# Retention's gate projected by tokens, and group norm's gains applied before the turn

## The chip, the cores and the metric

The kernel runs on one core of a Trainium2 chip. The metric is the device time of one execution in microseconds (us). Engines are named as in the profile: PE is TensorE's matmuls, PEld its weight loads, DVE VectorE, ACT ScalarE, POOL GpSimd, SP SyncE, whose queue issues nearly all transfers.

## The reference

Two layers over 256 tokens of width 1024 in float32. Each layer runs three token mixers side by side on a normalised input (MLA, MoBA and retention), merges them through sigmoid gates, multiplies by an output matrix and adds the result to the input; then comes a squared-ReLU MLP. Retention, which the change touches, is cut to this:

```python
p = h @ w_in                       # rq, rk, rv, rg are columns of p
...
o = (inner + cross).reshape(B, H, S, Dv)          # H = 4 heads, Dv = 128
mu = jnp.mean(o, axis=-1, keepdims=True)
var = jnp.mean(jnp.square(o - mu), axis=-1, keepdims=True)
o = (o - mu) * lax.rsqrt(var + GN_EPS)
o = o.transpose(0, 2, 1, 3).reshape(B, S, RET_V_W) * gn_w + gn_b
return jax.nn.silu(g) * o                         # g is rg, 512 columns
...
sigmoid(g_ret) * (o_ret @ w_branch_ret)
```

## The kernel before

**Data.** The 256 tokens are two tiles of 128 (t = 0, 1). The normalised input xn lies with the 1024 features along partitions, in 8 pieces k of 128. Every float32 product of weights is made of three fp32r products (`three`, L215): both operands are split into a high and a low part, and high x high, high x low and low x high are added in PSUM. Weights come from memory in blocks of 512 KB (`raw`, 4 buffers, issued on SP's queue at L180); ACT copies the high part (`whi`, L195), DVE subtracts for the low part (`wlo`, L197), 6 buffers each. `weight_plan` fixes the order of the blocks.

**Two ways to project.** `project` holds a 128 x 128 piece of xn still and moves 512 columns of weights: the result has tokens along partitions, one PSUM bank (`acc`, 4 of them) for each token tile. `project_t` holds a piece of weights still and moves the 256 tokens: the result has features along partitions. Retention's gate (`rg_unit`) uses `project_t`, in four blocks of 128 columns, two to a PSUM bank.

**Retention, in the order of the program.** The projections rqk and rv; the turns and scores of the heads (`ret_turn`, `ret_scores`); the gate rg, between whose four units the scores and values (`ret_values`, into the PSUM tiles `por`) are set; then the MoBA branch (bmoba0, bmoba1), with `group_norm` behind its second unit; then the gates gret0 and gret1, with `oret_turn` behind their first two units; then the retention branch bret0, bret1. `group_norm` normalises by tokens into `oret` (L826). `oret_turn` transposes it on PE (L840), so that features lie along partitions, applies the group norm's weight and offset there, a scalar for each partition (L844), multiplies by the gate (L845), and splits the result into high and low (L235, L236) for bret. The gate itself is scaled by the tokens' inverse norm laid along the free axis (`xn.row`, L861), passed through tanh (L862) and completed to silu (L863; the factor 0.5 is in L845).

**Order.** The program is a list of units (`prog`) with steps hung behind them (`at`, `slot`). A scheduler with a timeline of its own then orders the instructions of each engine, except where the code holds an engine to the program's order (`manual_schedule`, `keep_in_program_order`). Each engine executes its list in order. The SBUF buffer `KK` holds the MLA keys, and in the last layer also the final norm's gains `gf`.

Of the kernel before, what the change touches and what calls it, by code (L numbers as in the profile page):

```python
# [7 lines left out]
F32 = mybir.dt.float32  # L8
F32R = mybir.dt.float32r
AF = mybir.ActivationFunctionType  # L10
ALU = mybir.AluOpType
AX = mybir.AxisListType

P = 128
D = 1024
S = 256
NT = S // P
L = 2
KD = D // P
# [10 lines left out]
RT_H, RT_K, RT_V = 4, 64, 128  # L30
# [4 lines left out]
C_RQK, C_RV, C_RG = range(1952, 2464), range(2464, 2976), 2976  # L35
# [10 lines left out]
def weight_plan():  # L46

    plan = []

    def block(key, name, kt, cols, per):  # L50
        for j in range(0, kt, per):
            plan.append(((*key, j // per), name, (j, per), cols))

    def span(c, n):
        return range(c, c + n)

    for l in range(L):
        if l == 0:

            plan.append(((l, "b0", 0), "w_in", (0, 1), C_MLA))  # L60
            plan.append(((l, "mq", 0), "w_in", (0, 1), C_MQ))
            for k in range(1, KD):
                plan.append(((l, "b0mq", k), "w_in", (k, 1), range(0, 928)))
        else:
            block((l, "b0"), "w_in", KD, C_MLA, 2)
            block((l, "mq"), "w_in", KD, C_MQ, 2)
        block((l, "mk"), "w_in", KD, C_MK, 2)
        block((l, "mv"), "w_in", KD, C_MV, 2)
        mv, plan = plan[-4:], plan[:-4]
        for i, (key, name, kt, cols) in enumerate(  # L70
            (("qrope", "mla_w_q_up", 2, C_QROPE), ("qnope", "mla_w_q_up", 2, C_QNOPE), ("kvup", "mla_w_kv_up", 1, C_KV))
        ):
            block((l, key), name, kt, cols, kt)
            plan.append(mv[i])
        plan.append(mv[3])
        for i in range(2):
            block((l, "gmla%d" % i), "w_in", KD, span(C_GMLA + 512 * i, 512), 2)
        for i in range(2):
            block((l, "gmoba%d" % i), "w_in", KD, span(C_GMOBA + 512 * i, 512), 2)
        for i in range(2):  # L80
            block((l, "bmla%d" % i), "w_branch_mla", 4, span(512 * i, 512), 2)
        block((l, "rqk"), "w_in", KD, C_RQK, 2)
        block((l, "rv"), "w_in", KD, C_RV, 2)
        for n in range(4):
            block((l, "rg", n), "w_in", KD, span(C_RG + P * n, P), KD)
        for i in range(2):
            block((l, "bmoba%d" % i), "w_branch_moba", 4, span(512 * i, 512), 2)
        for i in range(2):
            block((l, "gret%d" % i), "w_in", KD, span(C_GRET + 512 * i, 512), 2)
        for i in range(2):  # L90
            block((l, "bret%d" % i), "w_branch_ret", 4, span(512 * i, 512), 2)
        for n in range(KD):
            block((l, "wout", n), "w_out", KD, span(P * n, P), KD)
        for f in range(0, NF + 2, 2):
            for i in (f, f + 1) if f < NF else ():
                block((l, "up", i), "w_mlp_up", KD, span(P * i, P), KD)
            for i in (f - 2, f - 1) if 2 <= f <= NF - ENDS else ():
                plan.append(((l, "down", i, 0), "w_mlp_down", (i, 1), range(D)))
        for i in range(NF - ENDS, NF):
            plan.append(((l, "down", i, 0), "w_mlp_down", (i, 1), range(D)))  # L100
    at, offset = {}, 0
    for key, name, (j, n), cols in plan:
        at[key] = (offset, n, len(cols))
        offset += P * n * len(cols)
    return plan, at, offset
# [14 lines left out]

G_ATT, G_MLP = 0, L * KD
G_CQ = 2 * L * KD
G_GN = G_CQ + L * 3
G_END = G_GN + L * 2 * RT_H


@with_exitstack
def trunk(ctx: ExitStack, tc: tile.TileContext, gx, wts, consts, gfin, xtok, out):


    nc = tc.nc
# [4 lines left out]
    sb = ctx.enter_context(tc.tile_pool(name="sb", bufs=1))  # L136
# [66 lines left out]
    def acc_tile(name="acc"):  # L203
        return ps.tile([P, 512], F32, name=name, tag="acc", bufs=4)
# [4 lines left out]
    def w2k(name):  # L209
        return sb.tile([P, 512], F32, name=name, tag="w2k", bufs=W2K)  # L210
# [9 lines left out]
    def gain(c):  # L220
        return G[:, c : c + 1]

    def halves(tile_):
        return tile_.rearrange("p (two s) -> p two s", two=2)
# [9 lines left out]
    def split_plain(src, hi, lo):  # L234
        nc.scalar.activation(hi, src, AF.Copy)  # L235
        nc.vector.tensor_sub(lo, src, hi.bitcast(F32))  # L236
# [119 lines left out]
    def project_t(l, key, n, xn, o):  # L356

        wh, wl = load_w(l, key, n, 0)
        for k in range(KD):
            xh, xl = xn.k(k)  # L360
            three(o, wh[:, k, :], wl[:, k, :], xh, xl, k == 0, k == KD - 1)
# [166 lines left out]
    xn = Normed(G_ATT)  # L528
# [21 lines left out]
    prog, steps = [], {}  # L550

    def at(slot, step):
        steps.setdefault(slot, []).append(step)

    def slot(key, j):
        return [k for k, _ in prog].index((key, j))
# [9 lines left out]
    def layer(l, xn, before):  # L566

        c0 = []
        c, mla, mqkv, rqkv = {}, {}, {}, {}
# [161 lines left out]
        omlaT, omobaT, oretT = [], [], []  # L731
# [50 lines left out]

            return done

        rT, or_ps, aT, rg, oret = [], [], {}, [], []

        def ret_turn(i):
            pt = misc_tile("prt")
# [23 lines left out]
        def group_norm():  # L812
            for t in range(NT):
                o = w2k("oret")
                oret.append(o)
                st = sb.tile([P, RT_H, 6], F32, name="gst", bufs=2)
                mv = sb.tile([P, RT_H, 2], F32, name="gmv", bufs=2)
                ve = small("gve")
                for h in range(RT_H):
                    nc.vector.bn_stats(st[:, h, :], or_ps[t][:, RT_V * h : RT_V * h + RT_V])  # L820
                    nc.vector.bn_aggr(mv[:, h, :], st[:, h, :])
                nc.vector.tensor_scalar(ve[:, 0:RT_H], mv[:, :, 1], GN_EPS, None, op0=ALU.add)
                nc.gpsimd.tensor_tensor(ve[:, RT_H : 2 * RT_H], ve[:, 0:RT_H], neghalf[:, 0:RT_H], op=ALU.pow)
                for h in range(RT_H):
                    cs = slice(RT_V * h, RT_V * h + RT_V)
                    nc.vector.tensor_scalar(  # L826
                        o[:, cs], or_ps[t][:, cs], mv[:, h, 0:1], ve[:, RT_H + h : RT_H + h + 1],
                        op0=ALU.subtract, op1=ALU.mult,
                    )

        def oret_turn(i):
            if i == 0:
                oretT.extend((t4("oreth"), t4("oretl")))
            pt = misc_tile("pot")
            y = w2k("oy")
            for kk in range(2):
                k = 2 * i + kk
                cs = slice(S * kk, S * kk + S)
                for t in range(NT):
                    nc.tensor.transpose(  # L840
                        pt[:, (2 * kk + t) * P : (2 * kk + t + 1) * P], oret[t][:, P * k : P * k + P], ident
                    )
                g = G_GN + 2 * RT_H * l + k
                nc.vector.tensor_scalar(y[:, cs], pt[:, cs], gain(g), gain(g + RT_H), op0=ALU.mult, op1=ALU.add)  # L844
            nc.vector.scalar_tensor_tensor(y, y, 0.5, rg[i], op0=ALU.mult, op1=ALU.mult)  # L845
            split_plain(y, *(o[:, 2 * i : 2 * i + 2, :].rearrange("p k s -> p (k s)") for o in oretT))

        project(l, "rqk", xn, 512, ret_done("rqk"))
        project(l, "rv", xn, 512, ret_done("rv"))


        rg_acc = []

        def rg_unit(n):
            if n % 2 == 0:
                rg_acc.append(acc_tile())
            acc = rg_acc[-1]
            project_t(l, "rg", n, xn, acc[:, S * (n % 2) : S * (n % 2) + S])
            if n % 2:
                z, th = w2k("rg"), w2k("tg")  # L860
                nc.vector.tensor_mul(halves(z), halves(acc), xn.row[:, None, :].to_broadcast([P, 2, S]))  # L861
                nc.scalar.activation(th, z, AF.Tanh, scale=0.5)  # L862
                nc.vector.scalar_tensor_tensor(z, th, 1.0, z, op0=ALU.add, op1=ALU.mult)  # L863
                rg.append(z)

        for n in range(RT_H):
            prog.append((("rg", n), lambda n=n: rg_unit(n)))
        branch(l, "bmoba", omobaT, th_moba, merged)
        th_ret = gates(l, "gret", xn)
        order_out = ExitStack()  # L870
# [67 lines left out]
        accs = [acc_tile() for _ in range(4)]  # L938
# [56 lines left out]
        for f in range(0, NF, 2):  # L995
# [5 lines left out]
            for g in (f - 2, f - 1) if 2 <= f <= NF - ENDS else ():  # L1001
                w = load_w(l, "down", g, 0)
# [16 lines left out]
        if not last:  # L1019
            xn = Normed(G_ATT + KD * (l + 1))  # L1020
# [41 lines left out]
        for t in range(NT):  # L1062
            y = sb.tile([P, D], F32, name="y", tag="t4", bufs=T4)
# [11 lines left out]
            else:  # L1075

                sl, more = slice(P, 2 * P), misc_tile("plast")
                for half, o in enumerate((accs[3], more)):
                    cs = slice(512 + 256 * half, 768 + 256 * half)
# [18 lines left out]
                op0=ALU.add, op1=ALU.add,  # L1098
# [5 lines left out]
            if t:  # L1104
                nc.vector.scalar_tensor_tensor(y[:, cs], xr[:, t, cs], r, gf[:, 0, cs], op0=ALU.mult, op1=ALU.mult)
                cs = slice(512, 768)
            else:
                cs = right
# [105 lines left out]
```

## Time and profile before

| | |
|---|---|
| time, median of 3 runs | 844.61 us (844.55 to 844.74) |
| the profiled execution: its own time, its span | 844.61 us, 842.8 us |
| granted TensorE clock, mean | 0.999 |
| PE, DVE, ACT busy | 99%, 72%, 59% of the span |
| matmuls, DVE instructions, ACT instructions | 4555, 1187, 867 |
| moved by DMA | 150.08 MB |

Busy time of PE includes the drain of each matmul, so matmuls in a row overlap in the records; the distance between two starts is what one costs. The waits of an engine list what it waited for, in total, how often and at longest. The chain of waits is the work that ended last, followed back from the end. The busy time by stretch gives, for a window of the span, the busy time and count of each engine, the granted clock, the share of the DMA engines and the GB/s they moved.

### The profile page before, as it was taken

The page shows a single profiled execution, that of the slowest core. Times are in us where ns is not written, and L with a number is a line of the kernel's source. Part 1 is how long each engine was busy: PE and PEld are TensorE (multiplying, and loading weights), DVE is VectorE, ACT ScalarE, POOL GpSimd, SP SyncE. Part 2 cuts the span into 40 slices and gives each one's busy share as a digit, 9 for nine tenths or more (in the row PEclk, how much of TensorE's full clock was granted, in tenths as well). Part 3 has the DMA queues.
Part 4 walks back from the last instruction along what each step waited for, and adds up shares of the span by engine and source line. Part 5 has one row for each costly group of instructions (what it writes and reads, how often), then busy time and mean ns, then how long its engine had stood idle before and what let it go on. Part 6 is the DMA issues. An engine that isn't in the chain of part 4 may idle for free.

```text
span 842.8 us, 12495 instructions
## 1 busy us (share of the span) xinstructions
PE 834.7 (99%) x4555; PEld 717.5 (85%) x4555; DVE 606.1 (72%) x1187; ACT 498.7 (59%) x867; POOL 14.4 (2%) x23
## 2 busy tenths in 40 slices
PE   9999999999999999999999999999999999999996
PEld 7888888988998888888888888879889988888886
DVE  7887787787777666666588868867878766556664
ACT  7757766535556555555677667654456555555552
POOL 0000000010000000000000000000100000000000
PEclk9999999999999999999999999999999999999999
DMA  9765444545456656665366545455565565666641
GB/s 355 255 208 183 129 144 153 171 151 183 146 175 222 200 193 185 197 191 182 118 207 220 174 139 164 138 163 155 171 186 161 181 204 184 184 199 184 191 126 51
DMA packets 42397, 150.08 MB, mean 178 GB/s; under 512 B 4704, under 2 KB 5088, under 8 KB 42336
## 3 DMA queue, kind: packets, MB, share of 16 engines
q1 hardware_dynamic: 41760, 148.42, 56.0%
q8 instruction: 36, 0.59, 0.3%
q10 hardware_dynamic: 576, 0.87, 0.3%
q14 instruction: 25, 0.20, 0.1%
HBM read 148.22 MB, written 1.05 MB: 177 GB/s over the span
## 4 chain that ended last, share of the span: by engine, by line
PE 98%; issue 1%; DMA 0%; DVE 0%; ACT 0%; POOLq 0%; POOL 0%; DVEq 0%
PE acc L216 20%; PE acc L217 20%; PE acc L218 20%; PE pup L955 13%; PE pup L957 7%; PE acc L906 5%; PE ps_pt L433 1%; PE ps_s L739 1%; PE po L460 1%; PE ps_s L400 1%; PE acc L632 0%; PE acc L635 0%; PE acc L633 0%; PE po L462 0%; PE pmt L878 0%
## 5 line engine op out<-in xcount | busy, mean ns | idle before, releaser
L197 DVE TENSOR_TENSOR wlo<-raw,whi 128x1024 fp32r<-128x1024 f32 (+3 forms) x286 | 336.9, 1184 | 164.2 <-ACT whi L195 100.7
L195 ACT ACTIVATE whi<-raw 128x1024 fp32r<-128x1024 f32 (+3 forms) x286 | 292.4, 1026 | 197.4 <-PE acc L218 92.5
L216 PE MATMUL acc<-whi,xs 128*128 128x512 f32 (+1 forms) x352 | 139.5, 398 | 0.0
L217 PE MATMUL acc<-wlo,xs 128*128 128x512 f32 (+1 forms) x352 | 138.5, 393 | 0.0
L218 PE MATMUL acc<-whi,xs 128*128 128x512 f32 (+1 forms) x352 | 138.3, 394 | 0.0
L955 PE MATMUL pup<-xs,whi 128*128 128x512 f32 x496 | 121.5, 391 | 0.0
L955 PEld LDWEIGHTS pup<-xs,whi 128*128 128x128 f32 x496 | 92.2, 188 | 18.6
L216 PE MATMUL acc<-whi,sq 128*128 128x512 f32 (+1 forms) x256 | 99.8, 390 | 0.0
L217 PE MATMUL acc<-wlo,sq 128*128 128x512 f32 (+1 forms) x256 | 99.6, 389 | 0.0
L218 PE MATMUL acc<-whi,sq 128*128 128x512 f32 (+1 forms) x256 | 98.4, 388 | 0.0
L218 PEld LDWEIGHTS acc<-whi,xs 128*128 128x128 f32 x352 | 66.2, 188 | 12.9 <-issue 0.2
L216 PEld LDWEIGHTS acc<-whi,xs 128*128 128x128 f32 x352 | 66.1, 188 | 12.7 <-issue 0.2
L217 PEld LDWEIGHTS acc<-wlo,xs 128*128 128x128 f32 x352 | 66.3, 188 | 12.0 <-issue 0.2
L957 PE MATMUL pup<-xs,wlo 128*128 128x256 f32 x496 | 68.5, 283 | 0.0
L957 PEld LDWEIGHTS pup<-xs,wlo 128*128 128x128 f32 x496 | 65.8, 191 | 2.9
L966 ACT ACTIVATE relu<-relu 128x256 f32<-128x256 f32 x64 | 25.8, 409 | 55.1 <-DVE relu L965 55.1
L218 PEld LDWEIGHTS acc<-whi,sq 128*128 128x128 f32 x256 | 48.0, 188 | 9.9
L216 PEld LDWEIGHTS acc<-whi,sq 128*128 128x128 f32 x256 | 48.2, 188 | 9.1
L217 PEld LDWEIGHTS acc<-wlo,sq 128*128 128x128 f32 x256 | 48.2, 188 | 8.8
L422 ACT ACTIVATE prob<-prob,smx 128x128 f32<-128x128 f32 x64 | 28.4, 445 | 11.5 <-DVE smx L419 11.1
L906 PE MATMUL acc<-mTh,whi 128*128 128x256 f32 x128 | 32.0, 286 | 0.0
L906 PE MATMUL acc<-mTh,wlo 128*128 128x256 f32 x128 | 31.7, 283 | 0.0
(276 smaller groups left out, 1192.8 us busy)
## 6 DMA issues: line engine op xcount, KB each, us to landing
raw<-wts SPq DMA_DIRECT2D x264, 512.0 KB, 3.9
raw<-wts SPq DMA_DIRECT2D x7, 464.0 KB, 7.2
raw<-wts SPq DMA_DIRECT2D x4, 416.0 KB, 3.3
xrow<-xtok SPq DMA_DIRECT2D x4, 256.0 KB, 8.3
raw<-wts SPq DMA_DIRECT2D x3, 256.0 KB, 4.0
DEC<-consts SPq DMA_DIRECT2D x1, 768.0 KB, 7.1
x<-gx SPq DMA_DIRECT2D x1, 512.0 KB, 6.4
gf<-gfin SPq DMA_DIRECT2D x1, 512.0 KB, 4.4
```

The source lines that it names most:

```text
L195: nc.scalar.activation(hi[:, cs], raw[:, cs], AF.Copy)
L197: nc.vector.tensor_sub(lo[:, cs], raw[:, cs], hi[:, cs].bitcast(F32))
L216: nc.tensor.matmul(o, ah, bh, start=start, stop=False)
L217: nc.tensor.matmul(o, ah, bl, start=False, stop=False)
L218: nc.tensor.matmul(o, al, bh, start=False, stop=stop)
L400: nc.tensor.matmul(o, b if swap else a, a if swap else b, start=i == 0, stop=i == 1)
L422: nc.scalar.activation(p[:, a:b], p[:, a:b], AF.Exp, bias=m[:, 2 + i : 3 + i], scale=scale, accum_out=m[:, 4 + i : 5 + i])
L433: nc.tensor.transpose(pt[:, P * i : P * i + P], got["p"][:, src : src + P], ident)
L906: nc.tensor.matmul(acc[:, :S], a, b, start=i == 0 and ks[0] == 0, stop=i == len(jobs) - 1 and ks[-1] == KD - 1)
L955: nc.tensor.matmul(u, w, xm.both(k), start=k == 0, stop=False)
L957: nc.tensor.matmul(u[:, 0:S], w, xm.k(k)[0], start=False, stop=k == KD - 1)
L966: nc.scalar.activation(s, s, AF.Square)
```

## The change

The gate rg is projected by `project`: xn's pieces are held still and its 512 columns of weights move, so that the gate has tokens along partitions. Its weights come in the same four blocks of 512 KB, cut along k in place of columns. tanh reads the accumulator itself, with the token's inverse norm as a scalar for each partition. The group norm's weights and offsets come as a row of 1024 values repeated on all partitions, one transfer of 512 KB a layer into the buffer `KK`, issued behind the first unit of rqk. `group_norm` multiplies by the weights, adds the offsets and applies the gate (the factor 0.5 is in `xn.halfcol`), all by tokens. `oret_turn` only transposes and splits.

```diff
-        for n in range(4):
-            block((l, "rg", n), "w_in", KD, span(C_RG + P * n, P), KD)
+        block((l, "rg"), "w_in", KD, span(C_RG, 512), 2)
...
-G_GN = G_CQ + L * 3
-G_END = G_GN + L * 2 * RT_H
+G_END = G_CQ + L * 3
...
         def group_norm():
...
+                w, b = rg["gn"][:, 0:512], rg["gn"][:, 512:1024]
+                nc.vector.tensor_mul(o, o, w)
+                nc.vector.tensor_add(o, o, b)
+                nc.vector.scalar_tensor_tensor(o, o, xn.halfcol[t], rg[t], op0=ALU.mult, op1=ALU.mult)
 
         def oret_turn(i):
...
-            y = w2k("oy")
...
-                g = G_GN + 2 * RT_H * l + k
-                nc.vector.tensor_scalar(y[:, cs], pt[:, cs], gain(g), gain(g + RT_H), op0=ALU.mult, op1=ALU.add)
-            nc.vector.scalar_tensor_tensor(y, y, 0.5, rg[i], op0=ALU.mult, op1=ALU.mult)
-            split_plain(y, *(o[:, 2 * i : 2 * i + 2, :].rearrange("p k s -> p (k s)") for o in oretT))
+            split_plain(pt, *(o[:, 2 * i : 2 * i + 2, :].rearrange("p k s -> p (k s)") for o in oretT))
...
-        rg_acc = []
-
-        def rg_unit(n):
-            if n % 2 == 0:
-                rg_acc.append(acc_tile())
-            acc = rg_acc[-1]
-            project_t(l, "rg", n, xn, acc[:, S * (n % 2) : S * (n % 2) + S])
-            if n % 2:
-                z, th = w2k("rg"), w2k("tg")
-                nc.vector.tensor_mul(halves(z), halves(acc), xn.row[:, None, :].to_broadcast([P, 2, S]))
-                nc.scalar.activation(th, z, AF.Tanh, scale=0.5)
-                nc.vector.scalar_tensor_tensor(z, th, 1.0, z, op0=ALU.add, op1=ALU.mult)
-                rg.append(z)
-
-        for n in range(RT_H):
-            prog.append((("rg", n), lambda n=n: rg_unit(n)))
+        def rg_done(accs):
+            for t in range(NT):
+                z = rg[t] = w2k("rg")
+                nc.scalar.activation(z, accs[t], AF.Tanh, scale=xn.halfcol[t])
+                nc.vector.scalar_tensor_tensor(z, z, 1.0, accs[t], op0=ALU.add, op1=ALU.mult)
+
+        def load_gn():
+
+            rg["gn"] = sb.tile([P, 2 * RT_H * RT_V], F32, name="gn", tag="KK", bufs=1)
+            src = bass.AP(tensor=gn.tensor, offset=gn.offset + 1024 * l, ap=[[0, P], [1, 1024]])
+            tc.keep_in_program_order(nc.sync.dma_start(rg["gn"], src))
+
+        project(l, "rg", xn, 512, rg_done)
+        at(slot("rqk", 0), load_gn)
```

More of the change, by code (lines that the diff above doesn't have):

```diff
@@ L122, with trunk @@
 G_CQ = 2 * L * KD
-G_GN = G_CQ + L * 3
-G_END = G_GN + L * 2 * RT_H
+G_END = G_CQ + L * 3
 @with_exitstack
-def trunk(ctx: ExitStack, tc: tile.TileContext, gx, wts, consts, gfin, xtok, out):
+def trunk(ctx: ExitStack, tc: tile.TileContext, gx, wts, consts, gfin, gn, xtok, out):
     nc = tc.nc
@@ L783, in ret_done @@
             return done
-        rT, or_ps, aT, rg, oret = [], [], {}, [], []
+        rT, or_ps, aT, rg, oret = [], [], {}, {}, []
         def ret_turn(i):
@@ L834, in oret_turn @@
             pt = misc_tile("pot")
-            y = w2k("oy")
             for kk in range(2):
                 k = 2 * i + kk
-                cs = slice(S * kk, S * kk + S)
                 for t in range(NT):
@@ L1195 @@
         gains[:, G_CQ + 3 * l + 2] = a["mla_kv_norm"][l]
-        for i, name in enumerate(("ret_gn_w", "ret_gn_b")):
-            c = G_GN + (2 * l + i) * RT_H
-            gains[:, c : c + RT_H] = a[name][l].reshape(RT_H, P).T
     arrays = {
@@ L1204 @@
         "gfin": np.ascontiguousarray(a["final_norm"]),
+        "gn": np.stack([a["ret_gn_w"], a["ret_gn_b"]], axis=1),
         "xtok": np.ascontiguousarray(a["x"].reshape(NT, P, D).transpose(1, 0, 2)),
```

## The prediction

> **What bounds the kernel now.** I read the page first, then the waits of PE, then the chain of waits, then the busy time by stretch.
>
> ```profile
> span 842.8 us, 12495 instructions
> PE 834.7 (99%) x4555; PEld 717.5 (85%) x4555; DVE 606.1 (72%) x1187; ACT 498.7 (59%) x867; POOL 14.4 (2%) x23
> PE 98%; issue 1%; DMA 0%; DVE 0%; ACT 0%; POOLq 0%; POOL 0%; DVEq 0%
> PE warm L548 <- DVE zero L155: 1.4, 1, 1.4
> 156.00:171.40 15.40, 15.40 (x132) 15.36 (x131) 11.66 (x20) 8.37 (x11) 0.00 (x0) 1.00 0.50 168
> 182.00:206.00 24.00, 24.00 (x111) 19.67 (x110) 20.05 (x38) 11.67 (x13) 2.32 (x2) 1.00 0.60 197
> ```
>
> The first three lines say that the chain is TensorE almost alone. The fourth is the only line that the waits of PE contain: after the first 1.4 us PE never waits. The last two are stretches of layer 0 (length, then busy PE, PEld, DVE, ACT, POOL, granted clock, DMA share, GB/s): the gate's projection, and the group norm's stage. PE is busy through them at full clock, DVE 20 of 24 us. So the time is the sum of PE's issue intervals, and what the change does on DVE, ACT and the DMA queue counts only if it makes PE wait.
>
> A matmul's recorded duration includes its drain, so I price one by the distance between starts. In order of time:
>
> ```profile
> 156.15 0.28 PE L216 MATMUL acc<-xs,whi 128*128 128x256 f32 x1
> 158.90 0.28 PE L218 MATMUL acc<-xs,wlo 128*128 128x256 f32 x1
> 159.60 0.28 PE L217 MATMUL acc<-xs,whi 128*128 128x256 f32 x1
> L218 PE MATMUL acc<-xs,wlo 128*128 128x256 f32 x32 | 9.2, 286 | 0.0
> 183.06 0.39 PE L216 MATMUL acc<-whi,xs 128*128 128x512 f32 x1
> 188.50 0.39 PE L216 MATMUL acc<-whi,xs 128*128 128x512 f32 x1
> ```
>
> From 156.15 to 158.90 lie 23 steps of 256 columns: 2.75 / 23 = 0.1196 us. From 183.06 to 188.50 lie 24 steps of 512 columns: 5.44 / 24 = 0.2267 us. Two narrow matmuls take 0.239 us, one wide one 0.227: about 12 ns is fixed per matmul. The row with x32 is one of three alike (L216, L217, L218), so the projection has 96 matmuls in a layer.
>
> **The change part by part.** *The projection.* 4 column blocks x 8 k x 3 products = 96 matmuls of 256 columns (96 x 0.1196 = 11.48 us) become 8 k x 2 token tiles x 3 = 48 of 512 columns (48 x 0.2267 = 10.88 us). That is 0.60 us off PE's chain in each layer, 1.20 us in all. The columns moved are the same; only the fixed part is halved.
>
> Bounds: I do not know the spacing of the wide stream at this place. Behind single transposes it is slower:
>
> ```profile
> 192.59 0.27 PE L840 MATMUL pot<-K,oret 128*128 128x128 f32 x1
> 192.62 0.48 PE L216 MATMUL acc<-whi,xs 128*128 128x512 f32 x1
> 192.93 0.39 PE L217 MATMUL acc<-wlo,xs 128*128 128x512 f32 x1
> 195.81 0.39 PE L216 MATMUL acc<-whi,xs 128*128 128x512 f32 x1
> 197.19 0.39 PE L216 MATMUL acc<-whi,xs 128*128 128x512 f32 x1
> ```
>
> Six steps from 195.81 to 197.19 give 0.230. At 0.230 the gain is 0.44 a layer; at 0.2267, which the undisturbed rows give and to which this stream is nearest, 0.60. So 0.9 to 1.2 us in all, and I take 1.2.
>
> The Trainium skill ("TensorE: Matmul & The Clock Gate", Back-to-back issue gap) gives N / 2.4 + 2.5 ns for an isolated matmul, 109 and 216 ns here, so a fixed part of only 2.5 ns. By it the gain would be 96 x 109.2 - 48 x 215.8 = 125 ns a layer, 0.25 us in all, and the time about 844.4; the trace does not agree, with 120 and 227 ns.
>
> *What is threaded through the projection* (the scores and values of retention) stays, but now interrupts wide matmuls:
>
> ```profile
> 121.16 0.40 PE L216 MATMUL acc<-whi,omlah 128*128 128x512 f32 x1
> 121.40 0.22 PE L400 MATMUL ps_s<-stk 128*128 128x128 f32 x1
> 122.08 0.40 PE L218 MATMUL acc<-whi,omlal 128*128 128x512 f32 x1
> ```
>
> Between 158.90 and 159.60, and between 121.16 and 122.08, lie one group of four score matmuls (L400) and two matmuls of the stream. The group costs 159.60 - 158.90 - 2 x 0.12 = 0.46 us in the narrow stream and 122.08 - 121.16 - 2 x 0.227 = 0.47 in the wide one. No difference.
>
> *The gate on DVE and ACT, the group norm, the turn.* The 16 transposes (L840) of a layer stay 16; a single one costs 192.93 - 192.59 - 0.227 = 0.11 us as before.
>
> ```profile
> L861 DVE TENSOR_TENSOR rg<-acc,rrow x4: 692/693/693, 163.2 to 586.1; 128x512 f32<-128x512 f32 x4
> L844 DVE TENSOR_SCALAR oy<-pot,GX x8: 537/542/544, 195.2 to 618.4; 128x256 f32<-128x256 f32 x8
> L845 DVE SCALAR_TENSOR_TENSOR oy<-oy,rg x4: 683/688/692, 201.1 to 619.5; 128x512 f32<-128x512 f32 x4
> L506 DVE TENSOR_TENSOR th<-th x16: 678/689/694, 177.9 to 636.2; 128x512 f32<-128x512 f32 x16
> L479 ACT ACTIVATE th<-acc,half x24: 669/688/693, 67.7 to 621.6; 128x512 f32<-128x512 f32 x24
> L862 ACT ACTIVATE tg<-rg x4: 617/624/633, 163.9 to 587.0; 128x512 f32<-128x512 f32 x4
> ```
>
> Per layer DVE loses 2 x 0.69 (L861), 4 x 0.54 (L844) and 2 x 0.69 (L845) = 4.92 us, and gains 2 x (product, sum, gate) = 6 x 0.69 = 4.13 us by the rows of L506 and L845, which have the same shapes. The gate's last product (L863) and the split of the turned tile keep their shapes. ACT pays 2 x (0.688 - 0.624) = 0.13 us more, since tanh now reads PSUM. So DVE is relieved by 0.8 us a layer; off PE's chain this is worth nothing.
>
> A rule of the Trainium skill speaks against this part: "VectorE: DVE Perf Modes", Mode 2×_2P, lets an fp32 operation with a scalar per partition run at twice the rate of one with a second tensor, and the change turns the former into the latter. The trace does not bear that out for these instructions, which read PSUM: 542 ns for 256 columns against 689 ns for 512.
>
> *Where it moves on the chain.* The 4.1 us now lie ahead of the transposes:
>
> ```profile
> 189.56 1.38 DVE L826 TENSOR_SCALAR oret<-por,gmv,gve 128x128 f32<-128x128 f32 x4
> 205.68 0.69 DVE L236 TENSOR_TENSOR oretl<-oy,oreth 128x512 fp32r<-128x512 f32 x1
> 206.75 0.62 PE L218 MATMUL acc<-whi,oretl 128*128 128x512 f32 x2
> ```
>
> Both tiles are normalised at 190.94 and PE first turns one at 192.59. With 4.13 us and up to two weight splits of 1.23 us (L197) between, they come at about 195 to 197.5; the turn, the copy and the split then need some 5 us where now two scalings, a product, the copy and the split run until 206.4. The branch matmul that uses the result starts at 205.8, about 205.2 after the change. So it fits, if the scheduler sets the transposes later in PE's order. Behind a transpose that waits, all of PE's queue waits; that is rival A.
>
> *PSUM.* Both accumulators of the gate are now held until tanh and the product have read them. bmoba1 needs their banks 24 matmuls after bmoba0 starts, 24 x 0.227 = 5.4 us after the projection's end. Two tanh and two products are 2.7 us; with a weight copy, a weight split and a decay product between them (1.06 + 1.23 + 0.55) 5.5 us if all were in series. They aren't; I take no wait, at worst a few tenths.
>
> *The extra transfer and the queue it stands in.*
>
> ```profile
> raw<-wts SPq DMA_DIRECT2D x264, 512.0 KB, 3.9
> gf<-gfin SPq DMA_DIRECT2D x1, 512.0 KB, 4.4
> SPq L180 <- DVE wlo L197: 84.4, 29, 5.1
> 170.47 1.06 ACT L195 ACTIVATE whi<-raw 128x1024 fp32r<-128x1024 f32 x1 [2.93 <-PE acc L217]
> L739 PE MATMUL ps_s<-KK,Q x64: 272/328/383, 60.0 to 503.3; 128*128 128x128 f32 x32, 128*128 128x256 f32 x32
> ```
>
> Each layer gets one transfer of 512 KB more on SP's queue; gf, of the same form, lands in 4.4 us. Ahead of the weights it delays them by that at most. They have the lead: SP waits for DVE to free raw buffers, ACT waits 2.93 us for PE to free a whi buffer, and six such blocks of 12 x 0.227 = 2.7 us stand between conversion and use. Cost zero; without that cover 4.4 us a layer. Its buffer is that of the MLA keys, last read at 503.3 (layer 1), long before this stage, so no wait there. gf, in the same buffer, must now wait for the group norm of layer 1; it is needed 200 us later.
>
> *Sum.* The profiled execution took 844.61 us, which is also the median of the runs: 842.8 of span and 1.8 around it. 844.6 - 1.2 = 843.4 us, 0.14% less.
>
> **The rivals.** A change under 0.2%, 1.69 us, is about what a measurement of this kernel cannot tell from none.
>
> *A, slower: PE stands at the transposes.* The scheduler writes PE's order by its own costs. If it leaves the first transpose 1.65 us behind the old end of the normalisation, PE waits 4.13 - 1.65 = 2.5 us a layer: 844.6 - 1.2 + 5.0 = 848.4 us. It turns the sign at 0.6 us of wait a layer, and counts as slower at 1.45. For it: the new DVE work is the only thing that grew ahead of a PE instruction, at 84% DVE load. Against: PE waits nowhere now, though many such turns exist.
>
> *B, no gain: the wide stream runs at the disturbed spacing* of 0.239 us that two narrow ones take. Then 844.6. Against it: neither stretch of steps shown is that slow. (The isolated gap of the Trainium skill's TensorE page would give nearly this.)
>
> *C, another order of layer 1.* A group of four MLA scores takes 0.66 us together, and 0.43 for each half where it is split, 0.2 more:
>
> ```profile
> 490.30 0.66 PE ps_s L739 x4
> 481.26 0.43 PE ps_s L739 x2
> 153.81 0.66 PE prt L791 x6
> 214.17 0.44 PE pmt L878 x4
> 569.34 0.66 PE prt L791 x6
> 629.70 0.44 PE pmt L878 x4
> ```
>
> Four more such splits give 844.2; undoing the one gives 843.2. Against a large effect: from retention's turn to the merge's turn, the changed stage, both layers take 60.36 us (214.17 - 153.81, 629.70 - 569.34), though DVE and ACT are ordered differently in them.
>
> *D, a larger gain.* In the gate's stretch weight loads fill 15.36 of 15.40 us, elsewhere 20 of 24. If PE is held by them where it changes to retention's small matmuls, 7 groups x 0.05 us a layer come on top: 0.7 us, 842.7. Against: the groups cost 0.46 and 0.47 us in both streams.
>
> **How the numbers follow.** Forecast 843.4: 0.50, itself 843.2 to 843.9. D 0.16, C 0.12, B 0.10, A 0.12. Faster by over 0.2% (under 842.9) is D and a little of the forecast's edge: 0.19. Slower by over 0.2% (over 846.3) is A and a trace of C: 0.13. The rest, 0.68, is within. The range leaves out A and the far side of D: 842.4 to 845.2, which holds a small wait in one layer.
>
> **What would show it.** Right: 96 x 256-column rows of the gate replaced by 48 rows of 512 columns spaced 0.227; 4459 PE instructions; the waits of PE still only the first one; the stage from retention's turn to the merge's turn 59.8 us in both layers. Wrong: a wait of PE for oret or for the gate's accumulator, a gap before L840's rows, weights waiting for a DMA, or a spacing above 0.23.

## The result, and the profile after

| | before | after |
|---|---|---|
| time, median | 844.59 us (844.5 to 845.03, 6 runs) | 849.65 us (849.41 to 850.33, 6 runs) |
| ratio | | 1.0058, 95% interval 1.0048 to 1.0068 |
| span of the profiled execution | 842.8 us | 847.7 us |

The change made the kernel 5.06 us slower; the forecast was 1.2 us faster. The page of the changed kernel and the waits of its PE:

```profile
span 847.7 us, 12301 instructions
PE 835.4 (99%) x4459; PEld 712.5 (84%) x4459; DVE 605.3 (71%) x1183; ACT 498.1 (59%) x867; POOL 15.8 (2%) x23
...
PE acc L214 <- ACT oreth L233: 3.1, 2, 1.6
PE pmt L873 <- DVE th L504: 1.5, 4, 0.4
PE warm L546 <- DVE zero L153: 1.4, 1, 1.4
```

The 96 matmuls are gone (4555 to 4459), as forecast, and DVE is 0.8 us less busy in all, where 0.8 us a layer was forecast. The first two waits are new. Once a layer PE stands 1.6 us at the retention branch for the copy of the turned tile into its high part; twice a layer it stands 0.4 us at the merge's turn for the merged branches.

To place the loss I measure one stage in order of time: from the turn of retention's queries and keys to the first matmul of the MLP. Before, then after, layer 0:

```profile
149.73 0.27 PE L791 MATMUL prt<-K,rqk 128*128 128x128 f32 x1
241.54 0.40 PE L955 MATMUL pup<-xs,whi 128*128 128x512 f32 x1
```

```profile
149.44 0.27 PE L789 MATMUL prt<-K,rqk 128*128 128x128 f32 x1
243.94 0.40 PE L950 MATMUL pup<-xs,whi 128*128 128x512 f32 x1
```

That is 91.81 us before and 94.50 after: 2.69 us more. Layer 1 gives the same two numbers within 0.01 us. From the first turn of the MLA inputs to this stage (111.38 us), from the MLP of layer 0 to this stage in layer 1 (323.72) and from the MLP of layer 1 to the last matmul (178.93) the two kernels agree to 0.01 us. So 5.4 us, twice 2.69, are lost in this stage; the profiled execution started 0.3 us sooner, which hides a part. Inside the stage, in the order of time of the changed kernel, PE first, then DVE, then ACT:

```profile
202.70 0.38 PE L840 MATMUL pot<-K,oret 128*128 128x128 f32 x2
204.31 0.82 PE L840 MATMUL pot<-K,oret 128*128 128x128 f32 x6
206.68 0.50 PE L214 MATMUL acc<-whi,oreth 128*128 128x512 f32 x1 [1.55 <-ACT oreth L233]
...
197.55 0.74 DVE L831 SCALAR_TENSOR_TENSOR oret<-oret,half,rg 128x512 f32<-128x512 f32 x1
199.35 0.74 DVE L831 SCALAR_TENSOR_TENSOR oret<-oret,half,rg 128x512 f32<-128x512 f32 x1
207.31 1.28 DVE L234 TENSOR_TENSOR oretl<-pot,oreth 128x512 fp32r<-128x512 f32 x2
...
203.82 1.38 ACT L477 ACTIVATE th<-acc,half 128x512 f32<-128x512 f32 x2 [1.22 <-PE acc L216]
205.09 1.05 ACT L193 ACTIVATE whi<-raw 128x1024 fp32r<-128x1024 f32 x1
206.04 1.08 ACT L233 ACTIVATE oreth<-pot 128x512 fp32r<-128x512 f32 x2
```

Before, the last two transposes and the start of the branch lay like this:

```profile
201.53 0.38 PE L840 MATMUL pot<-K,oret 128*128 128x128 f32 x2
205.84 0.39 PE L216 MATMUL acc<-whi,oreth 128*128 128x512 f32 x1
```

In the changed kernel DVE has finished the tiles at 198.3 and 200.1 us. PE does not wait for them: it turns them only at 202.7 and 204.3, because its order has them there, the last six directly ahead of the branch. So nothing is left on PE to cover the copy (L233), which in ACT's order also stands behind two tanh and a weight copy. PE waits 1.55 us there. The low products of the branch follow later still, so the merged branches reach the merge's turn late:

```profile
213.66 0.62 PE L216 MATMUL acc<-whi,oretl 128*128 128x512 f32 x2
215.55 0.66 PE L873 MATMUL pmt<-K,th 128*128 128x128 f32 x4 [0.37 <-DVE th L504]
217.96 0.66 PE L873 MATMUL pmt<-K,th 128*128 128x128 f32 x4 [0.36 <-DVE th L504]
...
214.08 0.69 DVE L503 SCALAR_TENSOR_TENSOR th<-th,acc 128x512 f32<-128x512 f32 x1 [1.54 <-PE acc L216]
```

This second wait lies in PE's order as well: both low parts (L234) were ready at 208.6, but the low product that DVE waits for (L503) stands only at 213.66, 6.98 us behind the first matmul of the branch.

A second thing had moved. The last values of retention, which the group norm waits for, in order of time before and after:

```profile
178.07 0.39 PE L810 MATMUL por<-rv,retA 128*128 128x128 f32 x2
```

```profile
180.93 0.39 PE L808 MATMUL por<-rv,retA 128*128 128x128 f32 x2
```

Counted from the start of the stage, the last of them starts at 31.6 us in place of 28.5, 3.15 us later (2.9 on the two traces' own clocks). The wide projection itself is no slower; it is the scheduler that set the scores and values later between its units.

### The profile page after: what moved, and what is told of

Read it like the earlier page. It is cut to its first block, busy times and chain, and to the rows that moved or that the text cites. A ratio compares the mean times of both kernels' runs of the same rounds, so it can differ in the third digit from the quotient of the medians.

```text
span 847.7 us, 12301 instructions
## 1 busy us (share of the span) xinstructions
PE 835.4 (99%) x4459; PEld 712.5 (84%) x4459; DVE 605.3 (71%) x1183; ACT 498.1 (59%) x867; POOL 15.8 (2%) x23
## 4 chain that ended last, share of the span: by engine, by line
PE 97%; issue 1%; DVE 1%; ACT 0%; POOL 0%; POOLq 0%; DVEq 0%
PE acc L214 20%; PE acc L215 20%; PE acc L216 20%; PE pup L950 13%; PE pup L952 7%; PE acc L901 5%; PE ps_pt L431 1%; PE ps_s L737 1%; PE po L458 1%; PE ps_s L398 1%; PE acc L630 0%; PE acc L631 0%; PE acc L633 0%; PE pqk L757 0%; PE po L460 0%
## 5 line engine op out<-in xcount | busy, mean ns | idle before, releaser
L195 DVE TENSOR_TENSOR wlo<-raw,whi 128x1024 fp32r<-128x1024 f32 (+3 forms) x286 | 336.5, 1183 | 173.0 <-ACT whi L193 108.7
L214 PE MATMUL acc<-whi,xs 128*128 128x512 f32 (+1 forms) x384 | 151.6, 396 | 0.0
L215 PE MATMUL acc<-wlo,xs 128*128 128x512 f32 (+1 forms) x384 | 150.7, 392 | 0.0
L216 PE MATMUL acc<-whi,xs 128*128 128x512 f32 (+1 forms) x384 | 150.4, 392 | 0.0
L216 PEld LDWEIGHTS acc<-whi,xs 128*128 128x128 f32 x384 | 72.2, 188 | 14.1 <-issue 0.2
L214 PEld LDWEIGHTS acc<-whi,xs 128*128 128x128 f32 x384 | 72.1, 188 | 13.8 <-issue 0.2
L215 PEld LDWEIGHTS acc<-wlo,xs 128*128 128x128 f32 x384 | 72.2, 188 | 13.4 <-issue 0.2
```

What stands on the lines that cost most here:

```text
L195: nc.vector.tensor_sub(lo[:, cs], raw[:, cs], hi[:, cs].bitcast(F32))
L214: nc.tensor.matmul(o, ah, bh, start=start, stop=False)
L215: nc.tensor.matmul(o, ah, bl, start=False, stop=False)
L216: nc.tensor.matmul(o, al, bh, start=False, stop=stop)
```

## The experiments

Each was timed on a chip beside the kernel before. The first four had two theories to tell apart, work added ahead of the turn (1) or scores set late (2); what they left led to the later ones. "Stage" is the stretch just defined, in layer 0; layer 1 agrees to 0.02 us. "Cover" is the time from the last transpose of the turn (L840) to the first matmul of the retention branch.

| kernel | median us | ratio to before, 95% interval | stage us | cover us |
|---|---|---|---|---|
| before | 844.59 | | 91.81 | 4.20 |
| after | 849.65 | 1.0058 (1.0048 to 1.0068) | 94.50 | 1.83, 1.55 of it wait |
| projection alone | 845.83 | 1.0010 (1.0001 to 1.0019) | 92.31 | 3.77 |
| weights and offsets alone | 844.79 | 0.9996 (0.9987 to 1.0005) | 91.77 | 4.47 |
| after, gate's product alone | 843.18 | 0.9980 (0.9971 to 0.9989) | 91.29 | 5.15 |
| after, one product more | 850.05 | 1.0057 (1.0044 to 1.0070) | 94.26 | 1.61, 1.3 wait |
| after, folded | 843.34 | 0.9982 (0.9974 to 0.9991) | 91.25 | 2.62 |
| after, scores in pairs | 843.37 | 0.9983 (0.9974 to 0.9992) | 91.28 | 3.79 |
| after, all reliefs | 843.56 | 0.9984 (0.9975 to 0.9993) | 91.29 | 8.31 |
| projection alone, scores in pairs | 844.05 | 0.9990 (0.9981 to 0.9999) | 91.40 | 8.30 |
| after, turn set earlier | 843.79 | 0.9987 (0.9978 to 0.9996) | 91.25 | 2.86 |
| after, scores in pairs, turn set late | 849.73 | 1.0054 (1.0040 to 1.0067) | 94.23 | 1.61, 1.3 wait |

The kernel before measured 844.73 to 845.03 us (medians) beside the experiments, so compare by the ratios. The stage is free of the 1.3 us by which the profiled executions differ at their start.

**Projection alone.** The kernel before with these lines; the rest of its chain unchanged.

```diff
-        for n in range(4):
-            block((l, "rg", n), "w_in", KD, span(C_RG + P * n, P), KD)
+        block((l, "rg"), "w_in", KD, span(C_RG, 512), 2)
...
+        def rg_done(accs):
+            for t in range(NT):
+                z = w2k("rg")
+                nc.scalar.activation(z, accs[t], AF.Tanh, scale=xn.halfcol[t])
+                nc.vector.scalar_tensor_tensor(z, z, 1.0, accs[t], op0=ALU.add, op1=ALU.mult)
                 rg.append(z)
...
+        project(l, "rg", xn, 512, rg_done)
```

> The kernel before with the wide projection of the gate alone (48 matmuls of 512 columns); the group norm's weights, offsets and the gate are applied behind the turn as before, so the gate is multiplied in the wrong layout: its time is that of the projection, its values are not the reference's. Theory 1 (the work added between the normalisation and the turn makes the retention branch late): nothing is added there, so only the projection's gain is left, 844.6 - 1.2 = 843.4 us, within 0.5, and PE waits nowhere. Theory 2 (the wide projection makes the scheduler set retention's scores and values later, 181.0 in place of 178.2 us, and that alone makes the branch late): 848 to 850 us with PE waiting for the split retention output.

Measured 845.83 us, between the two. The scores were as late as in the changed kernel, and with the old chain behind the turn PE waited at the merge's turn:

```profile
PE pmt L869 <- DVE th L505: 0.8, 2, 0.4
```

**Weights and offsets alone.** The changed kernel with the gate as before:

```diff
-        block((l, "rg"), "w_in", KD, span(C_RG, 512), 2)
+        for n in range(4):
+            block((l, "rg", n), "w_in", KD, span(C_RG + P * n, P), KD)
...
-                nc.vector.scalar_tensor_tensor(o, o, xn.halfcol[t], rg[t], op0=ALU.mult, op1=ALU.mult)
...
-            split_plain(pt, ...)
+            y = w2k("oy")
+            nc.vector.scalar_tensor_tensor(y, pt, 0.5, rg[i], op0=ALU.mult, op1=ALU.mult)
+            split_plain(y, ...)
```

> The other part alone: the gate is projected by features as before (96 matmuls of 256 columns); the group norm's weights and offsets are applied by tokens ahead of the turn (4 more DVE instructions of 0.69 us a layer there), the gate behind it from PSUM. Theory 1: 4 instructions in place of 6 stand ahead of the turn, one of 0.69 us for each half behind it; PE waits, 846.5 to 850 us. Theory 2: as before, 844.6 within 0.5.

Measured 844.79, no difference from before, PE without a wait. Theory 1 in its plain form falls: 4 more instructions ahead of the turn cost nothing where the scores are early. The extra transfer of 512 KB is in this kernel too, so it costs nothing.

**The gate's product alone.**

```diff
-                w, b = rg["gn"][:, 0:512], rg["gn"][:, 512:1024]
-                nc.vector.tensor_mul(o, o, w)
-                nc.vector.tensor_add(o, o, b)
```

> The changed kernel without the group norm's weights and offsets (they are left out of the computation): of the three DVE instructions by tokens for each tile only the gate's product is left, 2.8 us a layer less ahead of the turn, more with the weight splits that stand between. Theory 1: PE's wait for the split output goes, 843.5 to 845.5 us. Theory 2: the scores and values stay late, 849 to 850 us.

Measured 843.18: with late scores but 4 DVE instructions fewer ahead of the turn the wait is gone, and the stage is 0.52 us shorter than before. Theory 2 in its plain form falls too.

**One product more.**

```diff
                 nc.vector.tensor_add(o, o, b)
+                nc.vector.tensor_mul(o, o, w)
```

> The changed kernel with the product by the weights done once more (the values change): 2 x 0.69 us more on DVE ahead of the turn in each layer. Theory 1: the branch comes later by that and by the weight splits between, 1.4 to 2.8 us a layer, so 852.4 to 855.3 us, with PE's longest wait grown by as much. Theory 2: no change, 849.7 within 0.5.

Measured 850.05, ratio 1.0057 against 1.0058. More work ahead of the turn cost nothing more. That spoke against theory 1, and agreed with the rows above: at the branch, PE does not wait for DVE's products.

**Folded; scores in pairs; all reliefs; the projection with pairs.** Each loosens one or all of the delays.

```diff
-                nc.vector.tensor_mul(o, o, w)
-                nc.vector.tensor_add(o, o, b)
-                nc.vector.scalar_tensor_tensor(o, o, xn.halfcol[t], rg[t], op0=ALU.mult, op1=ALU.mult)
+                gw, gb = folded[t]
+                nc.vector.tensor_mul(o, o, gw)
+                nc.vector.tensor_add(o, o, gb)
...
+                nc.vector.scalar_tensor_tensor(gw, z, xn.halfcol[t], w, op0=ALU.mult, op1=ALU.mult)
+                nc.vector.scalar_tensor_tensor(z, z, xn.halfcol[t], b, op0=ALU.mult, op1=ALU.mult)
```

> The changed kernel with the gate multiplied into the weights and the offsets while the scores run, so that only one product and one sum of 0.69 us for each tile are left behind the normalisation (same result, 2 DVE instructions a layer more in all, 2 fewer ahead of the turn); the scores stay as late as in the changed kernel. Theory 3 (two delays add up: the scores set some 3 us later by the scheduler, and 4 of the 6 new products ahead of the turn; either alone fits into the time before the retention branch): most of the wait goes, 843.5 to 846 us. Theory 4 (only the count of DVE instructions in the stage matters): 849.5 or more.

```diff
-            at(slot("rg", 0) + h, lambda h=h: ret_scores(h))
-            at(slot("rg", 1) + h, lambda h=h: ret_values(h))
+            at(slot("rg", 0) + h // 2, lambda h=h: ret_scores(h))
+            at(slot("rg", 1) + h // 2, lambda h=h: ret_values(h))
```

> The changed kernel with the same instructions, but the scores of heads 0 and 1 behind the gate's first unit and of heads 2 and 3 behind its second (values one unit later), so that the last values stand 6 us of PE's work earlier in PE's order (19.5 in place of 25.4 us of matmul time behind the turn of the queries and keys). Theory 3: PE's wait for the split retention output goes with no DVE instruction taken away, 843.2 to 844.6 us. Theory 4, or a theory in which the products alone decide: 848 to 850 us.

"All reliefs" has both edits, and the normalisation on ACT:

```diff
+                nb = small("gnb")
...
-                    nc.vector.tensor_scalar(o[:, cs], or_ps[t][:, cs], ...)
+                    nc.scalar.activation(
+                        o[:, cs], or_ps[t][:, cs], AF.Identity, bias=nb[:, h : h + 1], scale=ve[:, RT_H + h : RT_H + h + 1]
+                    )
```

> All three reliefs at once on the changed kernel (same result): gate folded into weights and offsets, the normalisation itself on ACT (8 activations a layer with a scale and a bias for each partition in place of 8 DVE instructions), scores in pairs. Theory 3: no wait of PE is left, and what remains is the projection's gain of 0.60 us a layer: 843.0 to 843.6 us, not less, since PE has nothing else to lose. Theory 4: 846 to 849 us.

> The projection alone (as in the earlier experiment with the gate in the wrong layout, chain behind the turn as before), with the scores in pairs. Theory 3: its loss came from the late scores alone, so the pure gain of the projection shows, 843.2 to 843.8 us. Theory 4: 845.5 to 846, as without the pairs.

Measured 843.34, 843.37, 843.56 and 844.05 us: either relief alone removes the whole loss, and three remove no more than one. The pairs take no DVE instruction away; they bring the last values 6 us forward, 25.7 us after the stage's start against 31.6. The projection alone now gains, stage 91.40; so its loss came from the late scores. Its 844.05 us lie a little over the range of theory 3, and its stage gains 0.41 us where the others gain 0.52 to 0.57. The scores in pairs, the waits of PE, and the turn in order of time:

```profile
PE warm L546 <- DVE zero L153: 1.4, 1, 1.4
...
200.28 0.38 PE L840 MATMUL pot<-K,oret 128*128 128x128 f32 x2
200.72 0.82 PE L840 MATMUL pot<-K,oret 128*128 128x128 f32 x6
```

**The turn's place alone.** Up to here one could still say that the tiles are late in the changed kernel. The edits of the last two runs move nothing but the place of the transposes in PE's order. The first is the changed kernel, with PE's order held from the second unit of gret1 on and the turn put behind its third:

```diff
+        held = ExitStack()
+        at(slot("gret1", 1), lambda: held.enter_context(tc.manual_schedule(engines={mybir.EngineType.PE})))
         for i in range(2):
-            at(slot("gret0", 0) + i, lambda i=i: oret_turn(i))
+            at(slot("gret1", 2), lambda i=i: oret_turn(i))
+        at(slot("gret1", 3), held.close)
```

> The changed kernel with the same instructions and the scores as late as there; only PE's order is held by hand from the second unit of gret1 on, so that the 8 transposes stand behind its third unit (46.7 us of matmul time behind the queries' and keys' turn) and not behind its last (49.5), right ahead of the retention branch. Theory 5 (the tiles are ready at 200.1 us on the chip; the scheduler's order of PE puts their transposes at 202.7 to 205.1 without need, and the copy to the high part then stands bare ahead of the branch): the wait of 1.55 us goes and no wait at the transposes takes its place, 843.2 to 844.5 us. Theory 6 (DVE is really late): PE waits at the transposes instead, 847 to 850 us.

The second holds the fast kernel with the scores in pairs in the same way, with the turn behind the fourth unit.

> The kernel with the scores in pairs, which was fast, with PE's order held by hand so that its 8 transposes stand behind the last unit of gret1, right ahead of the retention branch, as in the changed kernel. Theory 5: the wait for the split output comes back although no DVE instruction is added and the tiles are ready early, 1.5 to 2.7 us a layer, 846.3 to 849.7 us. Theory 6: as without the hold, 843.4 within 0.5.

Measured 843.79 us and 849.73 us. The turn set earlier, its waits of PE and then its rows:

```profile
PE warm L546 <- DVE zero L153: 1.4, 1, 1.4
...
199.67 0.75 DVE L831 SCALAR_TENSOR_TENSOR oret<-oret,half,rg 128x512 f32<-128x512 f32 x1
...
201.67 1.03 PE L840 MATMUL pot<-K,oret 128*128 128x128 f32 x8
205.29 0.39 PE L214 MATMUL acc<-whi,oreth 128*128 128x512 f32 x1
210.28 0.62 PE L216 MATMUL acc<-whi,oretl 128*128 128x512 f32 x2
...
202.83 1.07 ACT L233 ACTIVATE oreth<-pot 128x512 fp32r<-128x512 f32 x2
204.81 1.37 ACT L477 ACTIVATE th<-acc,half 128x512 f32<-128x512 f32 x2 [0.91 <-PE acc L216]
```

and set late, with its waits of PE:

```profile
196.00 1.41 DVE L831 SCALAR_TENSOR_TENSOR oret<-oret,half,rg 128x512 f32<-128x512 f32 x2
...
205.09 1.03 PE L840 MATMUL pot<-K,oret 128*128 128x128 f32 x8
207.46 0.50 PE L214 MATMUL acc<-whi,oreth 128*128 128x512 f32 x1 [1.34 <-ACT oreth L233]
...
204.61 1.37 ACT L477 ACTIVATE th<-acc,half 128x512 f32<-128x512 f32 x2 [0.98 <-PE acc L216]
206.82 1.08 ACT L233 ACTIVATE oreth<-pot 128x512 fp32r<-128x512 f32 x2
...
PE acc L214 <- ACT oreth L233: 2.7, 2, 1.3
PE pmt L873 <- DVE th L504: 1.5, 4, 0.4
```

With the instructions and the late scores of the changed kernel, turning at 201.67 gives no wait at all, though the last product ends at 200.4. With tiles ready at 197.4, 7.7 us ahead of the transposes, the late place brings back both waits in the size of the changed kernel. Theory 5 stands (849.73 is just over the upper end of its range), theory 6 falls. ACT's order was not held, and followed: with the turn set earlier the copy (L233) runs ahead of the two tanh (L477), with the turn set late behind them, as in the changed kernel. The low product that DVE waits for comes 4.99 us behind the start of the branch (210.28) in place of 6.98, so the second wait goes with the first. Holding the order costs nothing in itself, since the first of the two is held as well.

## Why the prediction was wrong

**The projection's gain was right.** Forecast 0.60 us a layer. In the five kernels with the wide projection and the product by tokens in which PE doesn't wait, the stage is 0.52 to 0.57 us shorter than before (91.24 to 91.29, against 91.81); in the projection alone with the scores in pairs it is 0.41 us shorter. The wide stream of the changed kernel runs at 0.228 us, 23 steps in 5.25 us:

```profile
154.24 0.39 PE L216 MATMUL acc<-whi,xs 128*128 128x512 f32 x1
159.49 0.40 PE L215 MATMUL acc<-wlo,xs 128*128 128x512 f32 x1
```

48 x 0.2283 = 10.96 us in place of 11.48 gives 0.52. The gain estimated from the isolated gap of the Trainium skill ("TensorE: Matmul & The Clock Gate", Back-to-back issue gap), 0.13 us a layer, does not agree with it. Two PSUM banks held longer and the transfer of 512 KB (5.0 us to land) cost nothing, as forecast. The DVE instructions were sized rightly too: the three ahead of the turn take 0.68, 0.68 and 0.74 us, forecast 0.69 each. One reading beside it was too quick: the rows of L844, which the prediction held against a faster rate for an operation with a scalar for each partition, read PSUM. On SBUF the trace before does show that rate: such an operation takes 347 ns for 256 columns and 486 for 512 (L1109), a product of two tensors 419 and 684 (L373): 0.54 ns for each column more, against 1.04. The forecast did not rest on it.

**The step that failed is "Where it moves on the chain".** It looked for a wait of PE at the transposes and checked that the tiles come in time. They came at 200.1, forecast 195 to 197.5. The scores and values had also moved, by 3.15 us, which the prediction had not seen (it took PE's order around the projection as given), and the normalisation ended at 192.96 in place of 190.94; and three weight splits (L195) stand among the products, where it allowed two. But even 200.1 was in time, and "it fits, if the scheduler sets the transposes later" was the wrong condition. The scheduler did set them later, by more than was needed, and that was the loss: 1.55 us at the branch for the copy behind the turn, which the old place had covered with 4.2 us of matmuls, and 0.73 us at the merge's turn behind it. Stepwise, from the stage's start to the branch 57.24 us against 55.53 with the turn set earlier, 1.71 more; in the branch 13.16 against 11.83, 1.33 more; then 0.21; 3.25 us a layer. Less the gain of 0.56 that makes the 2.69 measured. (The view counts a wait from the end of the drain before it, so between starts the two waits cost more than 1.55 and 0.73.)

**Rival A** had the right sign, nearly the size (848.4, measured 849.65) and the wrong mechanism: it put a price on transposes ahead of their data, and the loss came from transposes far behind it. That its size came near is luck. **Rival C**, another order of layer 1 before this stage, did not occur (323.70 to 323.72 us in all kernels). **B and D** fall with the stage's 0.52 to 0.57 us; the 0.05 us a group that D reckoned with comes from no row. The stretch named as the sign of being right, 59.8 us from retention's turn to the merge's turn, is what the chain of waits of the changed kernel with the turn set earlier shows, 213.62 - 153.84 = 59.78:

```profile
153.84 0.66 PE prt L789 x6
213.62 0.44 PE pmt L873 x4
```

**Open:** why the scheduler starts the turn 2.6 us after the second tile is ready and ends it 5 us after. Shown is that its place moves forward with fewer products ahead of it and with earlier scores; the costs that it reckons with were not seen. How much of the 1.55 us is ACT's queue (the copy starts 0.9 us after the last transpose) and how much the copy itself was not parted either, since ACT's order moved together with the turn. Nor was it followed why the scheduler sets the low products late in the branch when the turn is late, or why the projection alone with the scores in pairs gains only 0.41.

## What to carry to other kernels

Where PE never waits, a cheaper matmul form is worth its issue intervals; here that sum gave 0.60 us a layer, and 0.52 to 0.57 came (0.41 in one kernel). But where a scheduler writes the order of each engine, added work on an engine with time to spare moves other instructions: ask of each step behind the change not only whether its data are in time, but what work stands between it and its consumer; here PE waited where the turn stood directly ahead of the branch, and didn't with 2.3 us of matmuls or more between (the folded kernel has the least). A turn that PE can do early is cheap to hold by hand, and either that, or the gate folded into the weights and offsets ahead, or an earlier slot for the scores made the change 0.13 to 0.18% faster than before (by the stages alone 0.13%) in place of 0.58% slower.

## What the runs showed of the hardware

A product with a third tensor, scaled by a value for each partition (L831), takes 0.742 to 0.752 us, against 0.683 to 0.692 for the same operation with a constant (L845 before) and the same shape. Where PE waits for nothing after its first 1.4 us, more relief of DVE and ACT brought nothing (843.34 to 843.56 us).
